# Where small corrections, operand splits and weight loads stand in the queues of a two-block transformer kernel

## The chip, the cores and the metric

The kernel runs as one program on one core of one Trainium2 chip. The metric is the device time in microseconds; several runs are summed up by their median. The core has a matrix engine (TensorE, PE in the profile; its weight loads are PEld), three engines for the rest (VectorE = DVE, ScalarE = ACT, GpSimd = POOL), and a queue engine (SyncE = SP) that here issues most transfers. Each engine runs its own queue in order.

## The reference, cut to what matters

One sequence of 1024 tokens, width 1024, float32, goes through two blocks. The first is a sliding-window attention layer and then a pooling layer; the second, which gets 16 meta tokens ahead of the sequence, has neighbourhood attention and a gated recurrence side by side, an output matrix `w_o`, and an MLP. Three places count here. The pooling layer:

```python
u, z = jnp.split(h @ w_in, [POOL_WIDTH], axis=-1)
p = multiscale_pool(u)
m = jnp.einsum('bsgc,gcd->bsgd', p, w_mix).reshape(B, S, POOL_WIDTH) * scale
return (m * jax.nn.silu(z)) @ w_out
```

`multiscale_pool` takes, in four groups of 256 channels, the mean over the last 2, 4, 8 or 16 tokens, and subtracts `u`. The first tokens have fewer than that behind them, so their sum is divided by their own count. After the layer come the residual sum, the norm that ends the first block, and the norm that begins the second. In the second block:

```python
y_hg = hgrn2_branch(q_hg, z_f, z_b, i_hg, g_hg, lb_all[:, l], hg_norm[l]) @ w_hg_out[l]
mix = jax.nn.sigmoid(gate_na) * y_na + jax.nn.sigmoid(gate_hg) * y_hg
h = h + mix @ w_o[l]
m = rms_norm(h, norm_mlp[l])
```

## The kernel before

**Products.** A float32 product is made of three products of rounded parts: each operand is split into hi (a cast, mostly on ScalarE) and lo (the operand less hi, on DVE or GpSimd). `split_evac` (L117 to 119) is one such pair for a 128x1024 piece; `split_w` (L79, L80) and `split_group` (L275, L276) split weights, with lo on GpSimd. A large matrix product is made as a Strassen-like scheme of 2x2 blocks, seven block products instead of eight; its sums of blocks (S1 to S4 of the left operand, differences of the weights) are made on DVE, and results are collected by copies and adds out of PSUM banks. A bank must be copied or added away before PE's later products can take it.

**Pooling projection** (`project_pairs`, with class `Pooled`, L866 on). Eight pairs of 128-column blocks, even pairs for `u` and odd ones for `z` of the same group. In a pair, PE makes six products of twelve 128x512 matmuls, by the blocks A11, A12, S2, S1, S3, S4 and A22 of the activations: the first bank is copied to SBUF by ScalarE (`copy`, L900), the next is added to it by DVE (`add`, through `vec`, L226), and so on; after the adds of odd pairs ScalarE applies Silu (L910). The pooling itself is done between these in small steps, a list `todo` from which `copy`, `add`, `opened` and `last` take the next: doubled sums over tokens (`doubled`, L226), then `less_u` (the mean less `u`, with a correction of the first 16 tokens: two DVE instructions of 128x16, `first` and its subtraction), then `cut` (the pooled half is split, hi on ScalarE at L118, lo on DVE at L119). `mix` multiplies a group's two pooled halves by `w_mix` and by Silu(z), stores the blocks (`d_mA...`) for the next product, and makes S1 to S4 of them; S3 is written over the block m[0,0], of which a store has been issued.

**Pooled output projection.** `times` makes 48 matmuls of one block product; the order is A11, A12, S2, S1, S4, S3, A22. `add_p` adds a finished bank to the residual rows `X` (DVE) and, where the rows are done, takes squares on ScalarE and multiplies by the gain. `second_norms` turns sums of squares into scales by Newton steps on small tiles (L124 to 132), `Rows.scale` scales rows alternately on DVE (L308) and ScalarE, and `turn_half` transposes scaled rows on PE (L282). The first four rows are done after the S4 product, so their scaling and transposes overlap with the S3 and A22 products. Ahead of that, the code splits the operands of the S3 product (`o7`) and of the last one (`o4` is A22, `t4` are its weights), normalises the meta tokens, and, between the transposes, splits gate weights (`wg`).

**The w_o stage** has the same plan. `mixed(e, hf)` loads two columns of w_hg, multiplies, and blends with the gates; the loop over e = 0, 2, 4, 6 makes the second half of them and the S1 and S3 blocks, and `load_w11` issues the first w_o weights in it. Then come the seven products; `add_x` (L1750 on) adds to `X`, whose halves the profile calls Xa and Xb.

**Order.** A list scheduler orders each engine's instructions when the program is built. `tc.issue_after(ins)` puts the instructions of its block that run on the engine of `ins` behind `ins` in that engine's queue; it does not change instructions on other engines.

Of the kernel before, what the change touches and what calls it, by code (L numbers as in the profile page):

```python
# [19 lines left out]
P = 128  # L20
# [10 lines left out]
def fused_kernel(tc, a, out, stop=None, dbg=None):  # L31
# [797 lines left out]
    with ExitStack() as ph:  # L829
# [34 lines left out]
        class Pooled:  # L864
# [33 lines left out]
            def copy(self, p, key, ps):  # L898
                c_ = ea[:, p - 2, :] if p in EARLY and key == "11" else self.dst(p, key)
                nc.scalar.copy(out=c_, in_=ps)  # L900
# [6 lines left out]
            def add(self, p, key, c_, ps):  # L907
                added[:] = [vec(c_, c_, ps, ALU.add)]
                if p % 2 and (p, key) != (3, "11"):
                    nc.scalar.activation(out=c_, in_=c_, func=AF.Silu)  # L910
# [3 lines left out]
            def last(self, p, ps):  # L914
# [5 lines left out]
                else:  # L920
                    nc.scalar.copy(out=c_, in_=ps)
                if p in EARLY:
# [9 lines left out]
            def pooled(self, g, j):  # L932
# [10 lines left out]
                def less_u():  # L943
                    pr, c_ = u[:, 16:], cur[-1]
                    first = small.tile([P, 16], F32, name="first", bufs=2)
                    vec(first, c_[:, 16:32], cnt[:, g, :], ALU.mult)
                    vec(pr[:, :16], first, u[:, 16:32], ALU.subtract)
# [3 lines left out]
                def cut():  # L951
                    self.pp[q][j] = s_tile(F32R)[:, :T], u_tile(F32R)[:, :T]
                    split_evac(*self.pp[q][j], u[:, 16:])
# [6 lines left out]
        def mix(g, q):  # L960
# [18 lines left out]
            for n, c_, x_, y_, op in (("S3", m[0, 0], m[0, 1], m[0, 0], ALU.subtract),  # L979
                                      ("S2", s2, m[1, 1], m[0, 0], ALU.add), ("S1", s1, m[0, 1], m[1, 1], ALU.add),  # L980
# [128 lines left out]
        with tc.issue_after(added[0].ins):  # L1109
            o7 = split_a("xl1", in_two(ring["S3"]))  # L1110
            o4 = split_a("xh1", in_two(ring["A22"]))
            mj = ea[:, 1:, :].rearrange("p a b -> p (a b)")
# [4 lines left out]
        ops = o7, split_b(w12)  # L1117
        t4 = list(zip(*[in_two(mp.tile([P, 4, 512], F32R, name=n, bufs=b)) for n, b in (("ub", 3), ("w22", 1))]))
        with tc.issue_after(made[0].ins):
            for i in range(2):  # L1120
                split_evac(*t4[i], w21[i])
        add_p(C, 0, 1, True)
        scaled = second_norms(0, 4)
        wg = []

        for n, ks in enumerate(((), (), (), (0, 1, 2), (3, 4), (5, 6), (7,), ())):
# [10 lines left out]
            if n in (1, 4):  # L1137
                wg.append(w_cols(w2, 4096 + len(wg) * P))
# [592 lines left out]
    with ExitStack() as ph:  # L1731
# [18 lines left out]
        def add_x(banks, h, ch, first=True, done=False, rows=range(4)):  # L1750

            for i in rows:
                t = 4 * h + i
                dst = X.at(t, ch)
                if first:
                    nc.vector.scalar_tensor_tensor(out=dst, in0=dst, scalar=rfin[:, t:t + 1], in1=banks[i], op0=ALU.mult,  # L1756
                                                   op1=ALU.add)
                else:
                    nc.vector.tensor_tensor(out=dst, in0=dst, in1=banks[i], op=ALU.add)
# [19 lines left out]
        for e in range(0, KT, 2):  # L1779
            if e == 6:  # L1780
                w11 = load_w11(wv)
            mixed(e, 1)
# [6 lines left out]
            if e == 4:  # L1789
                load_d(w21, wv, 1, 0)  # L1790
# [11 lines left out]
        o4 = split_a("xh1", in_two(a22))  # L1802
# [285 lines left out]
```

## Time and profile before

| | us |
|---|---|
| runs, median of 3 | 2376.18 (2375.15 to 2378.74) |
| profiled execution, whole time | 2372.9 |
| its span | 2371.1 |
| PE busy | 2277.2 |
| DVE busy | 1516.8 |
| ACT busy | 1021.4 |
| POOL busy | 776.1 |

The span is the time from the first to the last instruction in the profiled execution; the 1.8 us around it belong to the whole time. Busy is work of the engine itself, so a queue that stands still shows only as what is left. Starts below count from the span's begin. A row of the timeline has the start, the duration, the engine, the line of the kernel, the operation, out <- in, shapes and types, and in square brackets the time that the engine stood idle before it and what ended that. The pooling projection lies at about 505 to 660 us, the pooled output projection at 660 to 760, the w_o stage at 1600 to 1740.

### The profile page before, as it was taken

The numbers are of one execution on the slowest core, as the hardware profiler recorded it, in microseconds if no ns is written. First come the engines' busy times: TensorE is split into PE (matmuls) and PEld (weight loads), VectorE is DVE, ScalarE is ACT, GpSimd is POOL, SyncE is SP. The second block draws the span as 40 slices with busy tenths as digits, with TensorE's granted clock in tenths as the row PEclk, the third lists the DMA queues.
The fourth block names the chain that finished last, engine by engine and source line by source line (L and its number), as shares of the span: only waits on it lengthen the run. The fifth ranks groups of instructions, "written<-read, shape, count | busy, mean of one in ns | idle before, by whom it ended". The sixth has DMA issues, their size and how long they took to land. (4 is left out here: it accounts for less than half of the span.)

```text
span 2371.1 us, 32238 instructions
## 1 busy us (share of the span) xinstructions
PE 2277.2 (96%) x11910; PEld 1894.1 (80%) x11910; DVE 1516.8 (64%) x2740; ACT 1021.4 (43%) x1921; POOL 776.1 (33%) x519
## 2 busy tenths in 40 slices
PE   7999999988998999999999999999999999999997
PEld 6877777867776888888988888887778888878886
DVE  5566676798688355554166656668885444686775
ACT  5344452543355354544232322422475555533334
POOL 2112123343522254332222112114314444454455
PEclk9999999999999999999999999999999999999999
DMA  5111103423371222211111111358136444754231
GB/s 161 36 28 36 28 28 107 142 76 120 100 251 72 85 59 54 61 51 59 45 45 50 49 59 39 121 186 306 63 129 200 151 147 170 274 209 172 104 125 71
DMA packets 248941, 253.09 MB, mean 107 GB/s; under 512 B 61064, under 2 KB 183006, under 8 KB 244944
## 3 DMA queue, kind: packets, MB, share of 16 engines
q1 hardware_dynamic: 239968, 233.38, 30.2%
q10 hardware_dynamic: 8224, 16.00, 1.8%
q0 software_dynamic: 592, 1.65, 0.3%
q8 instruction: 94, 1.54, 0.3%
q14 instruction: 63, 0.52, 0.1%
HBM read 181.26 MB, written 69.46 MB: 106 GB/s over the span
## 5 line engine op out<-in xcount | busy, mean ns | idle before, releaser
L108 PE MATMUL mm<-xh,whi 128*128 128x512 f32 (+2 forms) x1616 | 622.0, 385 | 19.9 <-DVE z L226 6.2
L110 PE MATMUL mm<-xl,whi 128*128 128x512 f32 (+2 forms) x1616 | 615.2, 381 | 0.0
L111 PE MATMUL mm<-xh,wlo 128*128 128x512 f32 (+2 forms) x1616 | 612.8, 379 | 2.0 <-POOL wlo L80 2.0
L80 POOL TENSOR_TENSOR wlo<-wraw,whi 128x1024 fp32r<-128x1024 f32 (+1 forms) x99 | 234.6, 2373 | 751.9 <-ACT whi L79 644.5
L108 PEld LDWEIGHTS mm<-xh,whi 128*128 128x128 f32 x1616 | 305.7, 189 | 78.8 <-DVE z L226 7.0
L111 PEld LDWEIGHTS mm<-xh,wlo 128*128 128x128 f32 x1616 | 305.6, 189 | 60.7 <-POOL wlo L80 3.0
L110 PEld LDWEIGHTS mm<-xl,whi 128*128 128x128 f32 x1616 | 306.0, 189 | 50.8
L111 PE MATMUL mm<-whi,xl 128*128 128x512 f32 (+1 forms) x752 | 271.2, 361 | 0.0
L79 ACT CAST whi<-wraw 128x1024 fp32r<-128x1024 f32 (+1 forms) x99 | 101.1, 1022 | 265.4 <-PE mm L110 145.5
L110 PE MATMUL mm<-wlo,xh 128*128 128x512 f32 (+1 forms) x560 | 196.9, 352 | 2.7 <-POOL wlo L80 1.4
L108 PE MATMUL mm<-whi,xh 128*128 128x512 f32 (+1 forms) x560 | 196.6, 352 | 2.5 <-DVE x L527 1.0
L110 PE MATMUL mm<-wlo,xl 128*128 128x512 f32 x416 | 162.5, 391 | 7.3 <-POOL wlo L119 4.3
L108 PE MATMUL mm<-whi,xl 128*128 128x512 f32 x416 | 162.8, 391 | 6.0 <-DVE Xb L1756 2.4
L276 POOL TENSOR_TENSOR wlo<-raw,whi 128x1024 fp32r<-128x1024 f32 (+1 forms) x59 | 123.9, 2101 | 124.8 <-ACT whi L275 124.8
L111 PEld LDWEIGHTS mm<-whi,xl 128*128 128x128 f32 x752 | 141.8, 189 | 21.6
L110 PEld LDWEIGHTS mm<-wlo,xh 128*128 128x128 f32 x560 | 105.7, 189 | 17.8 <-POOL wlo L80 2.0
L108 PEld LDWEIGHTS mm<-whi,xh 128*128 128x128 f32 x560 | 105.8, 189 | 17.1 <-DVE x L527 1.4
L276 POOL TENSOR_TENSOR wlo<-wraw,whi 128x1024 fp32r<-128x1024 f32 (+1 forms) x28 | 69.0, 2466 | 135.0 <-ACT whi L275 96.6
L119 POOL TENSOR_TENSOR wlo<-wraw,whi 128x1024 fp32r<-128x1024 f32 x28 | 73.7, 2635 | 108.0 <-ACT whi L118 107.9
L108 PEld LDWEIGHTS mm<-whi,xl 128*128 128x128 f32 x416 | 78.1, 188 | 25.2 <-ACT whi L118 4.2
L110 PEld LDWEIGHTS mm<-wlo,xl 128*128 128x128 f32 x416 | 78.1, 188 | 25.1 <-POOL wlo L119 5.5
L2010 DVE TENSOR_TENSOR X<-X,mm 128x512 f32<-128x512 f32 x112 | 73.1, 681 | 38.2 <-PE mm L111 38.2
(436 smaller groups left out, 4581.7 us busy)
## 6 DMA issues: line engine op xcount, KB each, us to landing
wraw<-in_w_in_dram SPq DMA_DIRECT2D x48, 512.0 KB, 3.6
d_S<-st SPq DMA_DIRECT2D x64, 256.0 KB, 4.7
raw<-in_w_up_dram SPq DMA_DIRECT2D x30, 512.0 KB, 5.1
d_A<-st ACTq DMA_DIRECT2D x48, 256.0 KB, 2.0
fa<-d_S SPq DMA_DIRECT2D x10, 1024.0 KB, 4.7
fa<-d_A SPq DMA_DIRECT2D x9, 1024.0 KB, 4.8
wraw<-in_attn_w_in_dram SPq DMA_DIRECT2D x32, 256.0 KB, 3.0
xh<-in_w_down_dram SPq DMA_DIRECT2D x16, 512.0 KB, 5.4
```

The source lines that it names most:

```text
L79: nc.scalar.copy(out=hv[:, i:i + n], in_=view[:, i:i + n])
L80: nc.gpsimd.tensor_tensor(out=lv[:, i:i + n], in0=view[:, i:i + n], in1=f(hv[:, i:i + n]), op=ALU.subtract)
L108: nc.tensor.matmul(ps, lhsT=lh[0], rhs=rh[0], start=first and i == 0, stop=False, skip_group_check=chain)
L110: nc.tensor.matmul(ps, lhsT=lh[0], rhs=rh[1], start=False, stop=False, skip_group_check=chain)
L111: nc.tensor.matmul(ps, lhsT=lh[1], rhs=rh[0], start=False, stop=last and i == n - 1, skip_group_check=chain)
L119: return (lo_eng or nc.vector).tensor_tensor(out=lo, in0=src, in1=f(hi), op=ALU.subtract)
L276: nc.gpsimd.tensor_tensor(out=lv, in0=view, in1=f(hv), op=ALU.subtract)
L2010: added[:] = [nc.vector.tensor_tensor(out=dst, in0=dst, in1=banks[t], op=ALU.add)]
```

## The change

It touches three stages and no arithmetic.

*Pooling projection.* The two 128x16 corrections of `less_u` run on GpSimd instead of DVE (8 halves, so 16 instructions). `cut`'s ScalarE cast is queued behind the latest bank copy. S3 goes to a tile of its own. The Silu of pair 1's first block moves from the add to the pair's end.

*Pooled output projection.* The splits of the last product (`o4`, `t4`) move from ahead of the first rows' sums to behind them; the meta tokens' norm and the gate weights' splits are queued behind the scaling.

*w_o stage.* `mixed(6, 1)`, with its load, comes before `load_w11`; the splits `o4` and `t4` move behind the first rows' sums, and the DVE part of S3's operand split (`o7`) behind the adds of the product before.

```diff
             def copy(self, p, key, ps):
-                nc.scalar.copy(out=c_, in_=ps)
+                self.copied = nc.scalar.copy(out=c_, in_=ps).ins
...
-                if p % 2 and (p, key) != (3, "11"):
+                if p % 2 and (p, key) not in ((1, "11"), (3, "11")):
                     nc.scalar.activation(out=c_, in_=c_, func=AF.Silu)
...
+                if p == 1:
+                    c_ = self.dst(p, "11")
+                    nc.scalar.activation(out=c_, in_=c_, func=AF.Silu)
...
-                    vec(first, c_[:, 16:32], cnt[:, g, :], ALU.mult)
-                    vec(pr[:, :16], first, u[:, 16:32], ALU.subtract)
+                    nc.gpsimd.tensor_tensor(out=first, in0=c_[:, 16:32], in1=cnt[:, g, :], op=ALU.mult)
+                    nc.gpsimd.tensor_tensor(out=pr[:, :16], in0=first, in1=u[:, 16:32], op=ALU.subtract)
...
-                    split_evac(*self.pp[q][j], u[:, 16:])
+                    with tc.issue_after(self.copied):
+                        split_evac(*self.pp[q][j], u[:, 16:])
...
-            for n, c_, x_, y_, op in (("S3", m[0, 0], m[0, 1], m[0, 0], ALU.subtract),
+            s3 = s_tile()[:, :512]
+            for n, c_, x_, y_, op in (("S3", s3, m[0, 1], m[0, 0], ALU.subtract), ("S2", s2, m[1, 1], s3, ALU.add),
...
             o7 = split_a("xl1", in_two(ring["S3"]))
+        ops = o7, split_b(w12)
+        add_p(C, 0, 1, True)
+        with tc.issue_after(added[0].ins):
             o4 = split_a("xh1", in_two(ring["A22"]))
+            t4 = list(zip(*[in_two(mp.tile([P, 4, 512], F32R, name=n, bufs=b)) for n, b in (("ub", 3), ("w22", 1))]))
+            for i in range(2):
+                split_evac(*t4[i], w21[i])
+        scaled = second_norms(0, 4)
+        with tc.issue_after(scaled[1]):
             mj = ea[:, 1:, :].rearrange("p a b -> p (a b)")
...
-        ops = o7, split_b(w12)
-        t4 = list(zip(*[in_two(mp.tile([P, 4, 512], F32R, name=n, bufs=b)) for n, b in (("ub", 3), ("w22", 1))]))
-        with tc.issue_after(made[0].ins):
-            for i in range(2):
-                split_evac(*t4[i], w21[i])
-        add_p(C, 0, 1, True)
-        scaled = second_norms(0, 4)
...
-                wg.append(w_cols(w2, 4096 + len(wg) * P))
+                with tc.issue_after(scaled[0]):
+                    wg.append(w_cols(w2, 4096 + len(wg) * P))
...
         for e in range(0, KT, 2):
+            mixed(e, 1)
             if e == 6:
                 w11 = load_w11(wv)
-            mixed(e, 1)
...
-            if e == 4:
-                load_d(w21, wv, 1, 0)
+        load_d(w21, wv, 1, 0)
...
-        o4 = split_a("xh1", in_two(a22))
...
-        ops = split_a("xl1", in_two(a11)), split_b(w12)
-
-        t4 = list(zip(*[in_two(mp.tile([P, 4, 512], F32R, name=n)) for n in ("a22", "w22")]))
-        for i in range(2):
-            split_evac(*t4[i], w21[i])
+        with tc.issue_after(added[0].ins):
+            o7 = split_a("xl1", in_two(a11))
+        ops = o7, split_b(w12)
         wu0 = load_w(cols(w_up, 0))
         add_x(C, 0, 1, False, True)
+
+        with tc.issue_after(added[0].ins):
+            o4 = split_a("xh1", in_two(a22))
+            t4 = list(zip(*[in_two(mp.tile([P, 4, 512], F32R, name=n)) for n in ("a22", "w22")]))
+            for i in range(2):
+                split_evac(*t4[i], w21[i])
         scaled = X.norms(0, 4)
```

A scheduler sets the order on each engine, so the change shows best in what it makes of it. First ScalarE in the pooling projection, from the last copy of pair 6 on into pair 7 (`u` and `z` are the pairs' results, `sum` takes the hi part of a pooled half, `raw` and `wraw` are weights). Before:

```order
L921 COPY u<-mm 128x512
L900 COPY z<-mm 128x512
L118 CAST sum<-u 128x1024
L275 CAST whi<-raw 128x512
L910 ACTIVATE z<-z 128x512
L118 CAST sum<-u 128x1024
L900 COPY z<-mm 128x512
L79 CAST whi<-wraw 128x512
L900 COPY z<-mm 128x512
L910 ACTIVATE z<-z 128x512 x2
```

After:

```order
L921 COPY u<-mm 128x512
L900 COPY z<-mm 128x512
L275 CAST whi<-raw 128x512
L910 ACTIVATE z<-z 128x512
L900 COPY z<-mm 128x512
L79 CAST whi<-wraw 128x512
L900 COPY z<-mm 128x512
L118 CAST sum<-u 128x1024 x2
L910 ACTIVATE z<-z 128x512 x2
```

Both casts of the pooled halves now stand behind pair 7's three bank copies, where one stood behind the first copy and one directly ahead of the second.

Next DVE in the pooled output projection, after the adds into the last bank group that come ahead of the S3 operand's split (`xl1`; `xh1` is A22's operand, `w22` its weights, `mm` a bank, `sum` the gain; hx1, r1 and w1 are the meta tokens' norm). Before:

```order
L119 TENSOR_TENSOR xl1_6789<-ub_6590,xl1_6789 128x1024 x2
L119 TENSOR_TENSOR xh1_6794<-ub_6381,xh1_6794 128x1024 x2
L141 TENSOR_SCALAR hx1_6801<-ss_6799 16x1
L119 TENSOR_TENSOR w22_6822<-w21_6330,ub_6821 128x1024
L124 TENSOR_SCALAR r1_6802<-hx1_6801 16x1
L119 TENSOR_TENSOR w22_6822<-w21_6330,ub_6821 128x1024
L128 SCALAR_TENSOR_TENSOR w1_6803<-r1_6802,hx1_6801 16x1
L226 TENSOR_TENSOR raw_6369<-raw_6369,mm_6672 128x512
L132 SCALAR_TENSOR_TENSOR r1_6802<-w1_6803,r1_6802 16x1
L226 TENSOR_TENSOR raw_6370<-raw_6370,mm_6673 128x512
```

After:

```order
L119 TENSOR_TENSOR xl1_6793<-ub_6594,xl1_6793 128x1024 x2
L226 TENSOR_TENSOR raw_6372<-raw_6372,mm_6676 128x512
L226 TENSOR_TENSOR raw_6372<-raw_6372,sum_6438 128x512
L226 TENSOR_TENSOR raw_6373<-raw_6373,mm_6677 128x512
L226 TENSOR_TENSOR raw_6373<-raw_6373,sum_6438 128x512
L226 TENSOR_TENSOR raw_6374<-raw_6374,mm_6678 128x512
L226 TENSOR_TENSOR raw_6374<-raw_6374,sum_6438 128x512
L226 TENSOR_TENSOR raw_6375<-raw_6375,mm_6679 128x512
L119 TENSOR_TENSOR xh1_6826<-ub_6384,xh1_6826 128x1024
L226 TENSOR_TENSOR raw_6375<-raw_6375,sum_6438 128x512
L119 TENSOR_TENSOR xh1_6826<-ub_6384,xh1_6826 128x1024
L119 TENSOR_TENSOR w22_6832<-w21_6333,ub_6831 128x1024 x2
```

The four rows' sums stand directly behind the S3 operand's split; the last product's splits have gone behind them, and the token norm out of this place.

Last SyncE in the w_o stage, at the loads of the last w_hg columns and the first w_o weights (`st` holds gates and branch outputs). Before:

```order
L60 DMA wraw<-in_w_hg_out_dram 128x4x128 x2
L1743 DMA st<-d_gate 128x512
L1744 DMA st<-d_y 128x512
L232 DMA wraw<-in_w_o_dram 128x2x512 x2
L1743 DMA st<-d_gate 128x512
L60 DMA wraw<-in_w_hg_out_dram 128x4x128
L1744 DMA st<-d_y 128x512
L60 DMA wraw<-in_w_hg_out_dram 128x4x128
```

After:

```order
L60 DMA wraw<-in_w_hg_out_dram 128x4x128 x2
L1750 DMA st<-d_gate 128x512
L1751 DMA st<-d_y 128x512
L60 DMA wraw<-in_w_hg_out_dram 128x4x128 x2
L232 DMA wraw<-in_w_o_dram 128x2x512
L1750 DMA st<-d_gate 128x512
L232 DMA wraw<-in_w_o_dram 128x2x512
L1751 DMA st<-d_y 128x512
```

The last two w_hg loads now come ahead of the two w_o loads, and the second of these one transfer later.

More of the change, by code (lines that the diff above doesn't have):

```diff
@@ L978, in mix @@
             s2, s1 = [ring[n][:, 3, :] for n in ("S2", "S1")] if q == 3 else (s_tile()[:, :512], m[0, 1])
-            for n, c_, x_, y_, op in (("S3", m[0, 0], m[0, 1], m[0, 0], ALU.subtract),
-                                      ("S2", s2, m[1, 1], m[0, 0], ALU.add), ("S1", s1, m[0, 1], m[1, 1], ALU.add),
+            s3 = s_tile()[:, :512]
+            for n, c_, x_, y_, op in (("S3", s3, m[0, 1], m[0, 0], ALU.subtract), ("S2", s2, m[1, 1], s3, ALU.add),
+                                      ("S1", s1, m[0, 1], m[1, 1], ALU.add),
                                       ("S4", m[1, 0], m[1, 0], s2, ALU.subtract)):
@@ L1755, in add_x @@
                 if first:
-                    nc.vector.scalar_tensor_tensor(out=dst, in0=dst, scalar=rfin[:, t:t + 1], in1=banks[i], op0=ALU.mult,
-                                                   op1=ALU.add)
+                    added[:] = [nc.vector.scalar_tensor_tensor(out=dst, in0=dst, scalar=rfin[:, t:t + 1], in1=banks[i],
+                                                               op0=ALU.mult, op1=ALU.add)]
                 else:
-                    nc.vector.tensor_tensor(out=dst, in0=dst, in1=banks[i], op=ALU.add)
+                    added[:] = [nc.vector.tensor_tensor(out=dst, in0=dst, in1=banks[i], op=ALU.add)]
                 if done:
```

## The prediction

> **What bounds the kernel now.** I read the page's engine table first, then TensorE's waits over the whole span, then the clock by stretches, and last the timelines of the waits in the three stages that the change touches. The engine table of the page gives busy time and share:
>
> ```profile
> span 2371.1 us, 32238 instructions
> PE 2277.2 (96%) x11910; PEld 1894.1 (80%) x11910; DVE 1516.8 (64%) x2740; ACT 1021.4 (43%) x1921; POOL 776.1 (33%) x519
> ```
>
> TensorE (PE) works 96% of the time, and its work stays the same here. So the change can only gain PE's idle time, and matmuls at a lowered clock. The PE waits give: who waits, for whom, total us, how often, the longest.
>
> ```profile
> PE mm L108 <- DVE z L226: 7.1, 3, 3.9
> PE mm L108 <- ACT z L900: 6.9, 2, 3.9
> PE mm L282 <- DVE raw L308: 5.5, 1, 5.5
> PE mm L108 <- DVE u L226: 3.4, 2, 1.7
> PE mm L110 <- DVE wlo L119: 3.3, 3, 1.8
> PE mm L108 <- DVE Xb L1756: 2.4, 2, 1.7
> PE mm L108 <- ACT whi L79: 2.3, 1, 2.3
> PE mm L111 <- POOL wlo L80: 2.0, 2, 1.7
> ```
>
> These rows hold 32.9 us. The z and u rows are the pooling projection, where a product waits until a bank of the one before is copied or added away; raw is the pooled output projection, whose transposes wait for normed rows; wlo on DVE, Xb, whi and wlo on POOL are mostly the w_o stage. A long wait costs more than itself, which the windows show (stretch, length, busy us and count of PE, weight load, DVE, ACT, POOL, then granted clock, DMA share, GB/s):
>
> ```profile
> 525.00:535.00 10.00, 7.05 (x24) 5.68 (x25) 9.93 (x13) 5.42 (x7) 4.08 (x3) 0.83 0.00 1
> 600.00:610.00 10.00, 8.68 (x38) 7.24 (x39) 5.31 (x8) 5.37 (x8) 3.86 (x3) 1.00 0.36 101
> 653.00:660.00 7.00, 5.12 (x16) 4.10 (x17) 1.98 (x4) 2.54 (x4) 1.88 (x2) 0.76 0.56 173
> 745.00:757.00 12.00, 7.38 (x34) 6.51 (x35) 10.65 (x21) 6.68 (x13) 2.29 (x1) 0.72 0.18 54
> 1634.00:1645.00 11.00, 7.95 (x27) 6.13 (x28) 8.59 (x9) 3.46 (x4) 6.95 (x4) 0.84 0.68 242
> ```
>
> After an idle of 3.9 us (first and third row) the clock is 0.83 over 10 us and 0.76 over 7: 10 x 0.17 or 7 x 0.24, 1.7 us of work lost each time. The 3.0 us idle of the second row left it at 1.00. The last row holds two shorter waits (2.3 and 1.7) close together and loses 11 x 0.16 = 1.8.
>
> **Pooling projection: three edits.** Their rows, DVE and ScalarE (ACT) and GpSimd (POOL) by start, duration, operation, and the wait ahead of it:
>
> ```profile
> 519.85 3.31 POOL L276 TENSOR_TENSOR wlo<-wraw,whi 128x1024 fp32r<-128x1024 f32 x1 [3.54 <-ACT whi L275]
> 520.83 2.37 DVE L226 TENSOR_TENSOR first<-sum,cnt 128x16 f32<-128x16 f32 x1
> 545.02 2.45 DVE L226 TENSOR_TENSOR z<-z 128x512 f32<-128x512 f32 x1 [2.00 <-DMA d_mA<-z]
> 566.87 0.50 PE L108 MATMUL mm<-xh,whi 128*128 128x512 f32 x1 [2.27 <-DVE z L226]
> 576.90 0.50 PE L110 MATMUL mm<-u,whi 128*128 128x512 f32 x1 [0.83 <-DVE u L119]
> 584.78 1.67 DVE L226 TENSOR_TENSOR z<-z 128x512 f32<-128x512 f32 x1 [2.85 <-DMA d_mA<-z]
> 599.74 1.04 ACT L118 CAST sum<-u 128x1024 fp32r<-128x1024 f32 x1 [5.45 <-DVE u L226]
> 600.69 0.58 ACT L900 COPY z<-mm 128x512 f32<-128x512 f32 x1
> 653.30 1.04 ACT L118 CAST sum<-u 128x1024 fp32r<-128x1024 f32 x1 [0.70 <-DVE u L226]
> 654.25 0.58 ACT L900 COPY z<-mm 128x512 f32<-128x512 f32 x1
> L838 POOL TENSOR_SCALAR cnt<-cnt 128x16 f32<-128x16 f32 x4 | 1.0, 252 | 0.2
> ```
>
> *Casts behind copies.* At 599.74 ScalarE had waited 5.45 us in its queue for a pooled half, and the bank copy of pair 5 stood behind it, with PE's next product. Tied behind the copy, the cast no longer blocks it: the wait of 3.0 in the 600 to 610 window goes, +3.0. Pair 7 has the same pattern at 653.30: without that cast the copy can run at about 652, once the Silu ahead of it, which waits for DVE's sum of the other bank, is done. Of its 3.9 I take 2.5 and leave 1.4; a wait of 1.4 should not pull the clock down where 3.0 did not, so of the 1.7 lost I take +1.6 besides. What waits instead is the cast, with the ScalarE work queued behind it (for pair 7 the two Silus and the casts of the next stage's operands); the mix that reads it has the rest of its pair's products in front of it.
>
> *S3 into a tile of its own.* The subtraction at 545.02 overwrote a block whose store was still under way (2.00 of waiting, then 2.45 running), and DVE's queue behind it holds the sum that frees pair 2's bank; at 584.78 it is 2.85, for pair 4. The u row's two waits (3.4 in sum) follow. With a free tile the subtraction starts when its inputs are there, at least 2.0 sooner, and the sum is then bounded by its own matmuls. I take +1.3 of each 1.7, +2.6, and nothing for pair 6, where the u row has no third wait. Bounds are 0 (the new tile waits for a slot instead) and 3.4. The Silu of pair 1 that moves to the pair's end costs nothing: ScalarE is busy 5.42 of the 10 us there.
>
> *Corrections on GpSimd.* Sixteen DVE instructions go, sixteen come to GpSimd. On DVE one of 128x16 could take 2.37, as at 520.83, because a GpSimd weight subtraction was running (519.85, 3.31 long). On GpSimd the nearest row is 0.25 (L838, the same size); the far bound is a weight subtraction's 3.31. I take 0.25. In pair 3 the corrections then stand ahead of the next weight subtraction, and the sum that ends the 2.27 at 566.87 comes about 1.9 sooner: +1.9. The mix waits 0.83 and a little before it; with the halves ready earlier, +1.1. In pair 1 (the 3.9) GpSimd and DVE alternate on their corrections and sums and nothing is saved: its wait and its clock stay, −0.5. Behind the corrections on GpSimd's queue stand weight subtractions, which PE needs only in the next pair.
>
> [...]
>
> Sum here: 3.0 + 2.5 + 1.6 + 2.6 + 1.9 + 1.1 − 0.5 = **12.2**; bounds from 5 (casts alone) to 15.
>
> **Pooled output projection.** DVE rows around the last two products:
>
> ```profile
> 724.82 2.34 DVE L119 TENSOR_TENSOR xh<-ub,xh 128x1024 fp32r<-128x1024 f32 x2
> 729.62 0.67 DVE L226 TENSOR_TENSOR raw<-raw,mm 128x512 f32<-128x512 f32 x1
> 742.48 0.69 DVE L226 TENSOR_TENSOR raw<-raw,sum 128x512 f32<-128x512 f32 x1 [1.54 <-ACT ea L1045]
> 744.97 2.33 DVE L131 TENSOR_TENSOR w<-w,hx 128x8 f32<-128x8 f32 x1
> 748.82 1.41 DVE L308 TENSOR_SCALAR raw<-raw,r 128x1024 f32<-128x1024 f32 x2
> ```
>
> The first rows' sums (729.62) stand behind two splits for the last product (724.82, 1.17 each) and, with the token norm, two more among them. And a 128x8 step of the Newton iteration took 2.33 at 744.97, where a whole 128x512 sum takes 0.69 (742.48): GpSimd was subtracting the gate weights that the change ties behind the scaling. With four splits (4 x 1.17 = 4.7) behind the sums and at least 1.6 (2.33 − 0.69) off the iteration, 6.3 in all, the scaling at 748.82 can start 5 sooner, at about 743.8, with 1.3 left for the sums' own wait on PE. The wait of 5.5 ends, +5.5. Of the 3.4 us of clock in the 745 to 757 window (12 x 0.28) I credit half a drop, +0.9, since PE goes on in short pieces there. The splits serve the last product, which starts one product of 48 matmuls later (8.68 / 38 = 0.23 each, 11 us): 4.7 fit. The gate weights, now behind the scaling, are used only after that last product, another 11 us: nothing. Sum **6.4**, bounds 2 (the squares on ScalarE, 1.54 of waiting at 742.48, still end last) to 9.
>
> **The w_o stage.** SyncE's issues, then the work:
>
> ```profile
> 1618.73 2.02 SPq L232 DMA_DIRECT2D wraw<-in_w_o_dram  x2
> 1627.73 0.37 SPq L60 DMA_DIRECT2D wraw<-in_w_hg_out_dram  x1
> 1634.24 1.05 ACT L79 CAST whi<-wraw 128x1024 fp32r<-128x1024 f32 x1 [9.85 <-DMA wraw<-in_w_hg_out_dram]
> 1650.59 4.54 DVE L119 TENSOR_TENSOR xh<-a,xh 128x1024 fp32r<-128x1024 f32 x2
> 1685.43 6.59 DVE L119 TENSOR_TENSOR xl<-fa,xl 128x1024 fp32r<-128x1024 f32 x3
> 1691.94 0.73 DVE L1756 SCALAR_TENSOR_TENSOR Xb<-Xb,rfin,mm 128x512 f32<-128x512 f32 x1
> 1696.34 1.21 DVE L119 TENSOR_TENSOR w<-st,a 128x1024 fp32r<-128x1024 f32 x1
> 1704.96 0.69 DVE L1759 TENSOR_TENSOR Xa<-Xa,mm 128x512 f32<-128x512 f32 x1 [2.03 <-PE mm L111]
> 1709.41 1.41 DVE L308 TENSOR_SCALAR Xa<-Xa,r 128x1024 f32<-128x1024 f32 x2
> ```
>
> *Loads.* The last w_hg weights were issued at 1627.73, behind the w_o load of 1618.73, and cast at 1634.24 after 9.85 of waiting. In w_o's place they leave 9 us sooner, and the waits of 2.3 (whi) and 1.7 (wlo) go: +4.0, and the clock of the last window, +1.6. Late next: the first w_o weights, two transfers that now leave one tile later, with a whole half product ahead of their use. [...]
>
> *Splits.* Xb's sums (1691.94) waited behind three splits of 6.59; two of these now follow: the 2.4 of the Xb row go. The xh1 splits leave the queue at 1650.59 (4.54), behind which DVE's weight splits come; of the 3.3 that PE waits for those, I take 1.2, a little over a third. The next product's operand, split later, may cost 0.3. [...] Sum 4.0 + 1.6 + 2.4 + 1.2 − 0.3 − 1.5 = **7.4**, bounds 3 to 10.
>
> Total 12.2 + 6.4 + 7.4 = **26.0**. The profiled execution took 2372.9, so 2346.9; it lies 3.3 below the median of the runs, 2376.2, and from that the forecast is **2350**.
>
> **The rivals.**
> 1. *The waits are passed on.* A freed sum only meets the next queue: pair 7's Silu, GpSimd's subtractions. For it: DVE is at 9.93 of 10 in the first window. Against: 5.31 and 1.98 in the two windows of the casts. Half of the pooling gain and 2 elsewhere go: 26 − 8 = 18, **2358**. Chance 0.20.
> 2. [...] Chance 0.12.
> 3. [...] Chance 0.05.
> 4. *It doesn't do what it says*: the scheduler and the queues hide it, e.g. SyncE issues the w_hg load no sooner since its tile is not free, and the remaining waits close up: **2376**. Against: two casts and a load plainly stand behind others now. Chance 0.04.
>
> **How the numbers follow.** Forecast 0.59, with its own bounds of 5 + 2 + 3 = 10 to 15 + 9 + 10 = 34 if all fell together; they won't, so 26 ± 9. About 0.2% (4.75 us) is what a measurement of this kernel can tell from no change. Range: from 26 + 8 (2342) to rival 1 with its own error of 8 (2366). Faster 0.59 + 0.20 + 0.12 = 0.91; same 0.04; slower 0.05.
>
> **What would show it.** In the profile after: no PE wait on z's copy (L900) near 600, one of 1.4 near 652, the clock there at 1.00; raw L308 gone from the list of waits; whi L79 and Xb gone in w_o, a new one on Xa's transposes of 1 to 2.5; no DMA wait ahead of S3; POOL corrections of about 0.25. Wrong if corrections take over 1.6, if DVE's sums still come where they came, or if PE's busy time rises.

## The result

The changed kernel took 2355.7 us (median of 4 runs, 2354.5 to 2357.1), the kernel before 2375.7 (4 runs, 2374.2 to 2378.7). The ratio is 0.9915, with a 95% interval of 0.9897 to 0.9932: 20 us faster. The forecast was 2350, so 26 us were forecast and 20 came. Its signs and most of its mechanisms held; several sizes did not.

The page of the changed kernel, against the two rows that the prediction begins with:

```profile
span 2354.9 us, 32237 instructions
PE 2281.8 (97%) x11910; PEld 1900.3 (81%) x11910; DVE 1504.1 (64%) x2724; ACT 1020.2 (43%) x1921; POOL 785.5 (33%) x535
```

The span lost 16.2 us in this pair of profiled runs, which lie 2.8 below and 1.0 above the medians of their kernels. PE's busy time rose by 4.6, at the same number of matmuls. The prediction had called such a rise a sign of being wrong, but it is no more work: the matmuls in the stretches at half clock kept PE busy for nearly twice as long (in this profile, 128x512 matmuls 0.43 us from start to start between 481 and 485, 0.23 between 471 and 475), and it met more of them. The granted clock was at half for 48.6 us against 42.5, and PE was busy in 35.5 of these against 27.4; half of that difference is 4.0 of the 4.6. PE's waits now (who waits, for whom, total us, how often, the longest):

```profile
PE mm L108 <- DVE z L226: 5.2, 3, 3.7
PE mm L110 <- DVE wlo L119: 3.3, 3, 1.8
PE mm L108 <- ACT whi L118: 3.2, 3, 1.7
PE mm L111 <- POOL u L881: 2.5, 1, 2.5
PE mm L282 <- DVE u L308: 1.9, 1, 1.9
...
PE mm L108 <- ACT z L900: 1.0, 1, 1.0
PE mm L108 <- DVE u L226: 1.0, 2, 0.8
...
PE mm L282 <- DVE Xa L308: 0.6, 1, 0.6
```

Gone are the 5.5 for raw, 5.9 of the 6.9 for z's copies, 2.4 of the 3.4 for u, and the rows of Xb, whi (L79) and, all but 0.2, wlo (L80). New are a wait of 1.9 for the last rows' scaling (u L308), one of 0.6 for Xa, 0.8 more for whi (L118), and 2.5 for "u L881", which has to do with chance and not with the change, as will be seen.

To see where the time came from, the span is cut at events that every trace has. The stretches are the pooling projection with the end of the stage ahead of it (first row), the last three products of the pooled output projection up to the gates' first results (second), and the w_o stage (third). Before, then after (stretch, length, busy of PE, weight load, DVE, ACT, POOL, the granted clock, DMA):

```profile
477.90:671.70 193.80, 172.78 (x729) 137.64 (x729) 150.17 (x166) 75.79 (x109) 75.05 (x42) 0.98 0.38 118
717.00:795.00 78.00, 66.14 (x312) 53.66 (x312) 58.12 (x113) 41.20 (x83) 17.96 (x8) 0.96 0.26 92
1594.00:1747.70 153.70, 142.06 (x636) 114.99 (x636) 123.87 (x160) 67.37 (x102) 50.22 (x21) 0.99 0.49 171
```

```profile
478.90:664.20 185.30, 174.43 (x728) 139.99 (x728) 146.64 (x150) 75.70 (x109) 89.19 (x56) 0.96 0.36 112
707.60:782.20 74.60, 67.32 (x313) 54.95 (x313) 56.88 (x113) 41.21 (x84) 18.08 (x8) 0.95 0.27 96
1583.40:1731.50 148.10, 139.98 (x637) 113.89 (x637) 118.74 (x160) 66.79 (x103) 45.46 (x21) 1.00 0.51 178
```

8.5, 3.4 and 5.6 us came from these three, and 1.9 from the 45 us between the first and the second (671.7 to 717.0 before is 45.3 long, 664.2 to 707.6 after 43.4): 19.4. The rest of the span, which the change does not touch, took 3.2 back in this profile. The measured 20 agrees with the sum of the stages; that this pair of profiles shows 16.2 is luck.

Part of that luck can be read in the clock. Ahead of 478 the two programs run the same code and both then have an idle of 2.3 us; before (first fence) the clock stayed at 1.00, after (second) it fell to 0.76 over 14 us:

```profile
476.00:490.00 14.00, 11.36 (x50) 9.09 (x51) 14.00 (x23) 9.39 (x16) 4.02 (x2) 1.00 0.84 225
```

```profile
477.00:491.00 14.00, 11.78 (x39) 9.22 (x40) 12.43 (x21) 8.17 (x14) 4.03 (x2) 0.76 0.87 225
...
528.00:538.00 10.00, 7.23 (x19) 5.73 (x20) 9.93 (x10) 4.37 (x6) 4.18 (x6) 0.66 0.00 0
...
1729.00:1749.00 20.00, 16.68 (x62) 12.74 (x61) 18.13 (x30) 14.32 (x24) 4.77 (x2) 0.83 0.45 136
```

14 x 0.24 = 3.4, 10 x 0.34 = 3.4, 20 x 0.17 = 3.4. The rows of before that the prediction quotes give 1.7 (525), 1.7 (653), 3.4 (745) and 1.8 (1634). The loss came in portions of 1.7 us, one or two at a time, and the wait of 2.3 at 478 cost none of them before and two after. In the table below the clock's share of a stretch is added up from short windows in the same way.

### The profile page after: what moved, and what is told of

It reads as the page before. It is cut to its first block, busy times and chain, and to the rows that moved or that the text cites. A ratio compares the mean times of both kernels' runs of the same rounds, so it can differ in the third digit from the quotient of the medians.

```text
span 2354.9 us, 32237 instructions
## 1 busy us (share of the span) xinstructions
PE 2281.8 (97%) x11910; PEld 1900.3 (81%) x11910; DVE 1504.1 (64%) x2724; ACT 1020.2 (43%) x1921; POOL 785.5 (33%) x535
## 4 chain that ended last, share of the span: by engine, by line
PE 60%; DVE 11%; issue 3%; DMA 2%; ACT 2%; POOL 1%; SPq 0%; DVEq 0%; ACTq 0%; POOLq 0%
PE mm L110 18%; PE mm L108 18%; PE mm L111 18%; PE A L1550 2%; PE PT L1314 1%; DVE xl L119 1%; PE S L1291 1%; DVE sum L226 1%; PE tp L1570 1%; DVE raw L226 1%; DVE s L1303 1%; DVE xh L119 0%; DMA st<-d_y 0%; ACT ea L1050 0%; PE mm L282 0%
## 5 line engine op out<-in xcount | busy, mean ns | idle before, releaser
L80 POOL TENSOR_TENSOR wlo<-wraw,whi 128x1024 fp32r<-128x1024 f32 (+1 forms) x99 | 233.7, 2364 | 738.1 <-ACT whi L79 673.7
L79 ACT CAST whi<-wraw 128x1024 fp32r<-128x1024 f32 (+1 forms) x99 | 101.1, 1022 | 258.1 <-PE mm L110 146.0
L119 POOL TENSOR_TENSOR wlo<-wraw,whi 128x1024 fp32r<-128x1024 f32 x28 | 73.7, 2636 | 108.9 <-ACT whi L118 86.9
```

Source lines behind the costliest of these rows:

```text
L79: nc.scalar.copy(out=hv[:, i:i + n], in_=view[:, i:i + n])
L80: nc.gpsimd.tensor_tensor(out=lv[:, i:i + n], in0=view[:, i:i + n], in1=f(hv[:, i:i + n]), op=ALU.subtract)
L119: return (lo_eng or nc.vector).tensor_tensor(out=lo, in0=src, in1=f(hi), op=ALU.subtract)
```

## The experiments

Each of the first eight puts one part of the change back or repeats the change; the last four alter it. They ran on three chips in groups of four; the kernel before took 2375.8, 2374.3 and 2372.2 us there (9 to 11 runs each), so "gain" is against the kernel before on the same chip. The intervals of the ratios are about ±0.13%, or 3 us, wide, so that two gains can differ by some 4 us by chance; the lengths of the stages tell finer. "Pooling", "output" and "w_o" are the three stretches of above, in us, and behind each in brackets what the lowered clock took of it.

| kernel | time | gain | ratio, 95% interval | pooling | output | w_o |
|---|---|---|---|---|---|---|
| before (first profile) | 2375.7 | | | 193.8 (3.4) | 78.0 (3.4) | 153.7 (1.7) |
| changed (first profile) | 2355.7 | 19.9 | 0.9915, 0.9897 to 0.9932 | 185.3 (6.8) | 74.6 (3.4) | 148.1 (0) |
| changed_again | 2354.2 | 20.1 | 0.9913, 0.9901 to 0.9926 | 184.1 (5.1) | 74.6 (3.4) | 149.0 (1.7) |
| casts_untied | 2363.5 | 12.3 | 0.9952, 0.9939 to 0.9964 | 193.2 (10.2) | 74.3 (1.7) | 148.9 (1.7) |
| corr_on_dve | 2359.2 | 16.7 | 0.9937, 0.9922 to 0.9952 | 189.5 (6.8) | 74.2 (1.7) | 150.1 (3.4) |
| s3_in_place | 2358.2 | 17.6 | 0.9927, 0.9915 to 0.9939 | 187.4 (6.8) | 74.2 (1.7) | 149.0 (1.7) |
| pool_out_before | 2358.7 | 17.1 | 0.9931, 0.9918 to 0.9945 | 182.2 (1.7) | 77.9 (3.4) | 149.6 (1.7) |
| wo_before | 2357.8 | 16.5 | 0.9924, 0.9912 to 0.9937 | 185.5 (5.1) | 74.2 (1.7) | 153.7 (1.7) |
| wo_load_before | 2356.6 | 17.7 | 0.9926, 0.9914 to 0.9938 | 182.6 (3.4) | 74.6 (1.7) | 152.4 (3.4) |
| gates_untied | 2355.9 | 18.4 | 0.9919, 0.9908 to 0.9931 | 185.2 (6.8) | 74.5 (1.7) | 150.9 (3.4) |
| norm_later | 2351.3 | 20.9 | 0.9911, 0.9897 to 0.9926 | 182.7 (3.4) | 70.7 (0) | 151.0 (3.4) |
| wo_splits_later | 2353.8 | 18.3 | 0.9923, 0.9911 to 0.9936 | 184.4 (5.1) | 74.6 (1.7) | 150.0 (3.4) |
| pair1_add_first | 2353.5 | 18.6 | 0.9924, 0.9911 to 0.9937 | 181.3 (1.7) | 74.6 (3.4) | 149.0 (1.7) |
| all_three | 2348.7 | 23.5 | 0.9901, 0.9888 to 0.9915 | 185.4 (6.8) | 70.7 (1.7) | 149.8 (3.4) |

Eight profiles share the changed kernel's pooling code: 182.2 to 185.5, 184.0 in the mean. Without the clock's share they lie between 178.3 and 180.5. So this stage is known to about 1 us once the clock is taken off, and to 2 with it. The output stretch behaves otherwise. Nine profiles have its changed code (all but before, pool_out_before, gates_untied, norm_later and all_three), and it is 74.2 to 74.6 long in each of them: three lost two portions there, and the six that lost only one have a wait of 1.0 to 1.1 more. There a portion that is not lost is not time gained.

### The change once more: changed_again

> The changed kernel itself once more, on the same chip as the next three, as their reference. Its first profile had granted clocks of 0.5 to 0.6 for some 7 us behind a 2.3 us idle at 478, where the kernel before had 1.00 behind the same idle. If that drop is chance (the code up to there is the same), some of this kernel's runs are about 3 us faster, near 2353, and the median lies between 2353 and 2357. If it belongs to the change, the same drop stands in this profile too.

2354.2 (2352.6 to 2354.7). The lowered clock behind 478 stood in this profile again, but with one portion instead of two (1.7). Of the other kernels eight, among them norm_later (1.7) and gates_untied (3.4), had one or two there; pool_out_before, with the same code up to there, had none, like the kernel before. So it is chance, though none is the rarer case; the last section shows where the wait fell in the profiles before and after.

### The casts: casts_untied

```diff
-                    with tc.issue_after(self.copied):
-                        split_evac(*self.pp[q][j], u[:, 16:])
+                    split_evac(*self.pp[q][j], u[:, 16:])
```

> The changed kernel without the tie of the pooled halves' ScalarE casts behind the bank copy, everything else kept. Forecast's theory: the tie bought 3.0 at pair 5, 2.5 at pair 7 and 1.6 of clock behind pair 7, so 7.1 us slower than the changed kernel (about 2363), with PE waits of about 3 at pair 5's S2 and 3.5 to 3.9 at pair 7's S3 product, both for the z copy of L900, and a granted clock below 0.9 after the second. Rival (the waits are passed on by DVE's queue, and the tie alone does little): under 3.5 us slower, with the two waits under 2 each.

7.7 less gain than the changed kernel; the forecast had 7.1. Both waits come back, for the copy of z:

```profile
599.61 0.51 PE L108 MATMUL mm<-s2h,whi 128*128 128x512 f32 x1 [2.09 <-ACT z L900]
...
654.47 0.50 PE L108 MATMUL mm<-s3h,whi 128*128 128x512 f32 x1 [3.56 <-ACT z L900]
```

Without the lowered clock the stage is 183.0, 4.2 longer than the changed kernel's mean of the two profiles (178.8); the rest of its 193.2 is clock, 10.2 against 5.1 and 6.8, with a portion behind each of the two waits, the one of 2.1 too. So the waits were worth 4.2, where 5.5 was forecast, and the clock 3.4, where 1.6 was. The mechanism is shown; that the sum is met so closely is partly luck.

### The corrections: corr_on_dve

```diff
-                    nc.gpsimd.tensor_tensor(out=first, in0=c_[:, 16:32], in1=cnt[:, g, :], op=ALU.mult)
-                    nc.gpsimd.tensor_tensor(out=pr[:, :16], in0=first, in1=u[:, 16:32], op=ALU.subtract)
+                    vec(first, c_[:, 16:32], cnt[:, g, :], ALU.mult)
+                    vec(pr[:, :16], first, u[:, 16:32], ALU.subtract)
```

> The changed kernel with the sixteen corrections of less_u back on DVE, everything else kept. Forecast's theory: they bought 1.9 at pair 3's A22 product and 1.1 at the mix and cost 0.5 at pair 1, so this kernel should be 2.5 us slower than the changed one (about 2358), with the wait before pair 3's A22 product back at 2 to 2.3 us from 1.0. [...] A trace of the changed kernel adds a doubt about pair 1: there a GpSimd weight subtraction started behind the corrections and held up a DVE weight sum for 2.85 us; with the corrections on DVE that sum should take 0.7 again.

3.4 less gain; the stage is 4 to 5 longer (189.5), 3.9 without the clock. The wait ahead of pair 3's A22 product is back, and larger than before the change:

```profile
568.25 0.53 PE L108 MATMUL mm<-xh,whi 128*128 128x512 f32 x1 [3.39 <-DVE z L226]
...
605.01 0.50 PE L108 MATMUL mm<-s3h,whi 128*128 128x512 f32 x1 [1.46 <-ACT z L900]
...
651.60 0.50 PE L108 MATMUL mm<-s3h,whi 128*128 128x512 f32 x1 [2.34 <-ACT z L900]
```

So the move bought time, though some of the corrections are long on GpSimd too. How they fare there in the changed kernel:

```profile
522.82 1.15 POOL L949 TENSOR_TENSOR first<-sum,cnt 128x16 f32<-128x16 f32 x1 [3.53 <-DVE sum L226]
...
564.20 3.43 POOL L949 TENSOR_TENSOR first<-sum,cnt 128x16 f32<-128x16 f32 x1 [5.26 <-DVE sum L226]
567.71 0.22 POOL L950 TENSOR_TENSOR u<-first,u 128x16 f32<-128x16 f32 x1
```

Of the sixteen, eight took 0.21 or 0.22, seven 1.06 to 1.24, one 3.43: mean 0.83. Beside the one of 3.43, which ends at 567.6, DVE ran a row of 128x1008 to 128x1039 sums from 564.05 on, and its next instruction, an add that reads a bank, started at 567.5. Nor have they become much shorter: before the change the sixteen took 0.16 to 2.37 on DVE, 0.90 in the mean. But what stands behind them on GpSimd is a weight split, and PE waits for none of these between 500 and 660, whereas on DVE they stood in front of the sums that free PE's banks.

### S3: s3_in_place

```diff
-            s3 = s_tile()[:, :512]
+            s3 = m[0, 0]
```

> The changed kernel with S3 written over its block again, everything else kept. Forecast's theory: the free tile bought 1.3 at each of two A22 products (pairs 2 and 4), so 2.6 us slower than the changed kernel, with DVE waiting 2 to 3 us for a store ahead of S3 and PE waits of about 1.5 at both products. Rival (the sum waits for its own matmuls or for DVE anyway): no difference over 1 us, and the two waits at 0.2 and 0.8 as in the changed kernel.

2.4 less gain. The waits ahead of the A22 products of pairs 2 and 4 are 1.7 and 2.8, against 0.2 and 0.7 to 0.8 in the two profiles of the changed kernel (the second is 0.7 to 1.5 in the others with its pooling code):

```profile
552.50 0.50 PE L108 MATMUL mm<-xh,whi 128*128 128x512 f32 x1 [1.69 <-DVE u L226]
...
589.54 0.79 PE L108 MATMUL mm<-xh,whi 128*128 128x512 f32 x1 [2.80 <-DVE u L226]
```

Not all of it stays: pair 3's wait of 1.0 is not there, the mix waits 0.6 for 1.1, and without the clock the stage is 180.6, 1.8 longer than the changed kernel's 178.8. And the stretch from this stage to the output's last products is 44.8 here, 43.4 in the changed kernel, with waits of 0.7 and 0.9 that the changed kernel has not or at 0.5. The free tile saved 1.4 there too, which no step had forecast.

### The output projection put back: pool_out_before

This puts the operand splits, the token norm and the gate weights of the pooled output projection where they were.

> The changed kernel with the whole pooled output projection as before, everything else kept. Forecast's theory: 6.4 us slower (about 2362), with the 5.5 us wait of the transposes for the scaled rows back. The trace of the changed kernel shows a new wait of 1.9 us for the last row's scaling behind the gate products; if that is the change's own cost (token norm and gate weights now lie among the last adds), it is gone here, and the net is 5.9 minus nothing. Rival (the transposes' wait is only moved on to the last rows): under 3 us slower.

```profile
703.20:781.10 77.90, 65.95 (x313) 53.59 (x313) 58.05 (x113) 41.16 (x84) 17.97 (x8) 0.96 0.26 92
```

77.9 against 74.6: 3.3, not 6.4, and 2.9 by time. The 5.5 us wait is back (735.85, raw L308), with two portions of lowered clock; the wait of 1.9 at the last rows is not there. That the change brings a wait of its own here was right. What makes it is asked by the next two.

### Who makes the new wait: gates_untied and norm_later

```diff
-                with tc.issue_after(scaled[0]):
-                    wg.append(w_cols(w2, 4096 + len(wg) * P))
+                wg.append(w_cols(w2, 4096 + len(wg) * P))
```

> The changed kernel with the gate weights' splits no longer queued behind the scaling, the token norm still behind it. The forecast priced the tie at nothing. From the changed kernel's trace: GpSimd's two weight subtractions (2.4 each) there hold up a 16x1 step (2.15) and the 16x1024 scaling (2.55) of the token norm on DVE, and the last row's scaling comes 1.9 late. If the tie makes that wait, it is gone here, and a Newton step of the first rows takes 2.3 again, with the first transposes later by about 1: 0 to 2 us faster. If the token norm makes it, the wait of 1.9 stays, and this kernel is the same or 1 to 2 slower.

In the changed kernel the tie looks guilty: a small step of the token norm and its scaling took 2.15 and 2.55 us on DVE, beside GpSimd's weight subtractions of 2.39 and 2.40, and the last row is scaled late.

```profile
735.67 2.39 POOL L80 TENSOR_TENSOR wlo<-wraw,whi 128x1024 fp32r<-128x1024 f32 x1 [10.89 <-ACT whi L79]
735.91 2.15 DVE L132 SCALAR_TENSOR_TENSOR r<-w,r 16x1 f32<-16x1 f32 x1
...
741.17 2.40 POOL L80 TENSOR_TENSOR wlo<-wraw,whi 128x1024 fp32r<-128x1024 f32 x1 [3.12 <-ACT whi L79]
...
741.57 2.55 DVE L1129 TENSOR_SCALAR sum<-sum,r 16x1024 f32<-16x1024 f32 x1
```

Untying them brought the wait down from 1.9 to 0.3, but others of 0.4 and 1.0 came in its place, and the stretch is as long (74.5). One step of the token norm still takes 2.2 there (at 737.05), beside a weight subtraction that runs from 736.80 on. Moving the norm instead, behind the stage's last add and after its loop:

```diff
-        with tc.issue_after(scaled[1]):
-            mj = ea[:, 1:, :].rearrange("p a b -> p (a b)")
...
+        with tc.issue_after(added[0].ins):
+            mj = ea[:, 1:, :].rearrange("p a b -> p (a b)")
```

> The changed kernel with the meta tokens' norm moved from behind the first rows' scaling to behind the last add of the stage. Theory: the norm's small steps, each of which could wait for a GpSimd weight subtraction, delayed the last rows' adds, and with them the last scaling; without them the 1.9 us wait there goes, and now and then a lowered clock behind it: 2 to 3 us faster than the changed kernel. Rival (the gate weights' subtractions would hold up any DVE work there, or the norm's steps now delay the last Newton iteration): the wait stays over 1, same time within 1.

```profile
704.20:774.90 70.70, 64.48 (x312) 52.05 (x312) 55.42 (x113) 41.00 (x84) 18.06 (x8) 1.00 0.28 101
```

70.7: 3.9 shorter, in this stretch, than the changed kernel, and free of a lowered clock in this run. all_three has the same edit and again 70.7, with one portion of lowered clock. Against the changed kernel's two profiles, 1.0 of the 3.9 is idle time of PE in norm_later and the rest clock; in all_three 1.9 is idle time. The wait of 1.9 (last scaling) is gone, and one of 1.1 for a transposed half (xl L322), which five of these kernels show between the transposes (gates_untied among them), is 0.2. What the norm cost can be read on DVE. Its nine instructions there, eight small steps and the scaling, took 5.9 us in the changed kernel, 4.7 of them in the two rows shown above; these end at 738.06 and 744.12, the weight subtractions beside them at 738.06 and 743.57. In norm_later, where GpSimd does nothing beside them, the nine took 2.1, with the scaling at 0.74:

```profile
750.97 0.74 DVE L1148 TENSOR_SCALAR sum<-sum,r 16x1024 f32<-16x1024 f32 x1
```

So the cost was the norm's place beside the gate weights' splits, in a queue that the rows' adds share. Moving the norm away is enough; untying the splits is not. By time, norm_later gains 20.9 on its chip against 20.1 and 19.9: a difference that the times alone can't show.

### The w_o stage put back: wo_before and wo_load_before

wo_before has the whole stage as before; wo_load_before only this:

```diff
-            mixed(e, 1)
             if e == 6:
                 w11 = load_w11(wv)
+            mixed(e, 1)
```

> The changed kernel with the whole w_o stage as before. Forecast's theory: 7.4 us slower than the changed kernel. From the changed kernel's trace: waits of 2.3 and 1.7 at the last mixed products and 1.7 and 0.7 at Xb back, one of 1.1 and one of 1.2 ahead of two split weights gone, and the 0.6 at the transposes gone: 2.3 + 1.7 + 2.4 - 1.1 - 1.2 - 0.6 = 3.5, and 1.8 of clock: 5.3. Rival (the gains pass on to the next wait): under 3.

153.7 against 148.1 and 149.0, and 3.6 less gain than changed_again: 4.7 to 5.6, by the stretch, nearer the 5.3 read from the trace than the 7.4 of the forecast.

> The changed kernel with only the order of the w_hg and w_o loads as before. Forecast's theory: 4.0 of idle back and a lowered clock behind it, 5.6 us slower than the changed kernel, less what the earlier w_o loads save. If two idles of 2.3 and 1.7, neither of them long, don't lower the clock, 4.0. Rival: the w_o weights' own splits then come sooner and the 1.2 and 1.1 us waits of the changed kernel at 1645 and 1652 go, so only 4.0 + 1.7 - 2.3 = 3.4.

152.4, 3.4 more than changed_again, of which 1.7 is clock; 2.4 less gain. The waits of the load, in this kernel, and those that the changed kernel has instead:

```profile
1620.24 0.50 PE L108 MATMUL mm<-xh,whi 128*128 128x512 f32 x1 [1.67 <-ACT whi L79]
1622.69 0.79 PE L111 MATMUL mm<-xh,wlo 128*128 128x512 f32 x1 [1.71 <-POOL wlo L80]
...
1654.33 0.50 PE L110 MATMUL mm<-wlo,xl 128*128 128x512 f32 x1 [1.62 <-DVE wlo L119]
```

```profile
1645.39 0.50 PE L110 MATMUL mm<-wlo,xl 128*128 128x512 f32 x1 [1.24 <-DVE wlo L119]
...
1652.56 0.50 PE L108 MATMUL mm<-whi,xl 128*128 128x512 f32 x1 [1.66 <-ACT whi L118]
1654.83 0.49 PE L110 MATMUL mm<-wlo,xl 128*128 128x512 f32 x1 [1.77 <-DVE wlo L119]
```

The rival's mechanism was the right one: with the load in time PE comes earlier to the next products, whose weights are split at the pace they had. Of the 4.0 that the load cost before the change, 2.3 meet PE again in this profile: a wait of 1.2 that was not there, and 1.7 where it was 0.6. The second stands in every profile with this code, the first is anything up to 1.4 and in some under 0.3. That the rival's 3.4 was met to the tenth is luck, since 1.7 of it is clock, for which it had no term.

### Three edits on top of the change

wo_splits_later puts the split of the last product's weights out of the Newton iteration, behind the scaling:

```diff
             o4 = split_a("xh1", in_two(a22))
+        scaled = X.norms(0, 4)
+        with tc.issue_after(scaled[1]):
             t4 = list(zip(*[in_two(mp.tile([P, 4, 512], F32R, name=n)) for n in ("a22", "w22")]))
             for i in range(2):
                 split_evac(*t4[i], w21[i])
-        scaled = X.norms(0, 4)
```

> The changed kernel with the two splits of the last w_o product's weights behind the scaling of the first rows, out of the Newton iteration. Theory: the transposes' wait of 0.6 us goes, with up to 1 us of spread around it; the splits are ready before the last product: 0.5 to 1 faster, hard to tell by time, to be seen in the trace. Rival: the splits are late for the last product and PE waits 1 or more for them there.

The 0.6 us wait of the transposes is gone and no other has come; without the clock's share the stage is 146.6, against 147.3 to 148.1 in the changed kernel. But corr_on_dve, with the wait and the same w_o code as the changed kernel, has 146.7, so a gain is not shown, and the time, 18.3 of gain, shows none either.

pair1_add_first ties pair 1's pooling steps behind the sum that frees its bank:

```diff
+                if p == 1 and key == "22":
+                    with tc.issue_after(added[0].ins):
+                        self.steps()
-                if p % 2 and key != "11":
+                elif p % 2 and key != "11":
                     self.steps()
```

> The changed kernel with pair 1's later pooling steps queued behind the sum that frees the bank for its last product. Theory: the 3.7 us wait before that product comes from four DVE steps that stand ahead of the sum, one of them held up by a GpSimd weight subtraction (2.85); with the sum first the wait falls under 1, and no lowered clock (0.5 for some 4 us) follows: 2.8 + 1.7 to 3.4 = 4.5 to 6 us faster than the changed kernel. Rival (the steps are only moved and the mix of the first group waits for its halves, or pair 2's sums wait): under 2 faster, with waits of 2 to 3 between 550 and 580.

The 3.7 us wait is gone, and the clock stays up there. In its place the first group's mix waits:

```profile
535.21 0.74 PE L108 MATMUL mm<-sum,whi 128*128 128x512 f32 x2 [2.26 <-ACT sum L118]
536.95 0.50 PE L110 MATMUL mm<-u,whi 128*128 128x512 f32 x1 [1.00 <-DVE u L119]
```

3.3 of 3.7 are given back within 5 us: the rival's case. What it saves is the clock, when it saves it: 1.7 was lost in this stretch, but 6.8 in all_three, which has the same edit and two portions behind the new wait.

> The changed kernel with the three last edits together (token norm later, w_o weight splits later, pair 1's sum first). Theory: their sum, 7 to 10 us faster than the changed kernel, 2346 to 2349. Rival (each gain is taken back by the next wait): under 4.

2348.7 (2348.0 to 2349.7) is the fastest kernel measured, 23.5 below the kernel before on its chip. The interval of its ratio overlaps the changed kernel's, so that it beats the kernel before is shown, and that it beats the changed one is shown in the output stretch (70.7) and not by the time. The expected 7 to 10 did not come. By gain it is 3.5; the output stretch gives 3.9, and the other two stretches (185.4 and 149.8) are as long as in the changed kernel.

## Why the prediction was right, and where its sizes were off

- **What bounds the kernel.** Right: all that was gained is PE's idle time and clock, and every stage's gain is made up of its waits and its clock.
- **Casts behind copies.** Right: the 3.0 at pair 5 went, 3.9 at pair 7 fell to 1.0 (1.4 was left in the sum), and the clock stays at 1.00 behind it. casts_untied gives 7.7 back; 7.1 was forecast, with two errors that cancel: the waits were worth 4.2 for 5.5, the clock 3.4 for 1.6.
- **S3.** Right: 1.7 to 0.2 and 1.7 to 0.8, 2.4 in all (2.6), of which s3_in_place gives 1.8 back in this stage. It also gave 1.4 later, through no step of the prediction.
- **Corrections.** The sign was right, the terms were not. Pair 3 gained 1.3 (1.9 was forecast). "The mix waits 0.83 and a little before it; with the halves ready earlier, +1.1" failed: it still waits 1.07, for the same split (u L119). Yet put back on DVE they cost 3.4 by time, more than their 2.5: pairs 5 and 7 then wait 1.5 and 1.3 more as well, which the prediction had not in its sum. "On GpSimd the nearest row is 0.25" was low: 0.83 in the mean. The mark of 1.6 each, at which the sixteen would use up the forecast 26 (26 / 16), was not reached, and the 13 us that the sixteen do take on GpSimd (16 x 0.83) are not on PE's path: it waits for none of GpSimd's work between 500 and 660. In pair 1 nothing was lost, 3.7 of waiting for 3.9.
- **Pooled output projection.** "+5.5" was right, and the splits' cover held. The half drop of clock, "+0.9", did not come in the two profiles of the changed kernel (3.4 lost, as before). "The gate weights, now behind the scaling, are used only after that last product: nothing" looked for the weights' user and not for who shares their engine and queue; the token norm that moves with them had no price at all. Beside each other they brought a wait of 1.9. That is 6.4 forecast and 3.4 measured; norm_later shows that 7.3 was there.
- **w_o.** The wait of the loads went ("+4.0"), and Xb's 2.4. But the step "of the 3.3 that PE waits for those, I take 1.2" misread its row and had the wrong sign. Of the row's 3.3 only 1.8 (at 1669.26) lies in w_o; 1.2 and 0.3 lie in the pooled output projection, at 694.27 and 671.66. And w_o's share grew by one of 1.2, and the one for whi ahead of it by 1.1, since PE came earlier to weights that are split no earlier. And "+1.6" for the clock came in one of two profiles only, by luck: behind the waits at 1652 and 1654 the clock fell again in changed_again and in all nine other kernels that have them. No run shows the term "−1.5" for the transposes; the changed kernel's list of waits has 0.6 there, and more than that is not shown. Of 7.4, 4.7 to 5.6 came.
- **Sum.** 12.2 + 6.4 + 7.4 = 26 was forecast; the stretches give 9.8 (by the mean of 184.0) + 1.9, 3.4 and 4.7 to 5.6, 20 to 21; the 1.9, between two stages, is in no step of the prediction. Rival 1, with 18, came nearer to the 20 than the forecast with 26, and its mechanism, waits passed on to the next queue, is what w_o's loads and the further edit of pair 1 show. It is not what the change met in the pooling projection, where most of it had been placed. Not tried alone were the Silu that moves in pair 1, priced at nothing, and w_o's splits.

## What to carry to other kernels

Price a moved instruction by who stands behind it in its new queue, and by what the other engines run beside it there, as well as by who needs its result: the token norm was needed much later, its scaling took 2.55 us beside a weight subtraction and 0.74 without one, and it still cost up to 4 us. A wait taken away ahead of a stage that is itself just in time is worth what the next supplier has in hand (2.3 of w_o's 4.0 came back, 3.3 of pair 1's 3.7), so read the next two waits on the same chain before adding up the first. And where the clock's losses differ from run to run by several portions, compare stage by stage, with the clock's share and without it, before believing a few microseconds.

## What the runs showed of the hardware

The lost clock came in portions: over 14 profiles, in the three stages, the sum of length x (1 - granted clock) behind a wait was 0, 1.7 or 3.4 us, nothing between. The length of a wait alone doesn't settle whether one follows: waits of 2.1 (casts_untied at 599.6) and 1.9 (changed kernel at 724.8) were followed by a lowered clock, while 3.0 at 601.3 before the change was not, and the same 2.3 at 478 was followed by none (before and pool_out_before), one (norm_later, all_three and others) or two portions (changed kernel, gates_untied) in runs of the same code.

Where the wait falls does, nearly, in the profiles before and after. In both the clock is at half for 3.41 or 6.83 us (but for the last microseconds of the program), and in each these stretches start on one grid of 3.413 us, to within 0.01 us: before, the first and the last of them start 2344.96 us apart, 687 steps of that grid. Nine of the other profiles, in windows of 3 us, fit such a grid to 0.03 us. Cut along the grid of its own profile, the 3.0 us wait before the change falls into two windows (first two rows: PE busy 1.68 and 2.12 of 3.41), and the 2.1 us wait of casts_untied into one (last two rows: busy 1.32, then half clock):

```profile
596.62:600.03 3.41, 1.68 (x8) 1.03 (x6) 3.41 (x3) 0.29 (x1) 3.05 (x1) 1.00 0.00 0
600.03:603.44 3.41, 2.12 (x9) 1.80 (x10) 3.41 (x6) 1.26 (x3) 0.00 (x0) 1.00 0.52 154
...
597.32:600.73 3.41, 1.32 (x6) 0.94 (x6) 2.22 (x2) 1.53 (x2) 3.41 (x3) 1.00 0.00 0
600.73:604.14 3.41, 3.41 (x10) 2.64 (x9) 2.82 (x4) 1.49 (x3) 1.81 (x2) 0.50 0.53 154
```

In the profiles before and after, cut this way from end to end, 13 of these windows at full clock have PE idle for 1.9 us or more, and half clock followed every one; it followed 1 of the 8 with 1.6 to 1.8 idle, 2 of the 60 with 0.6 to 1.6, and none of the others. The grid lies differently in time from run to run, which is the chance at 478: before, the idle time there fell into two windows with 1.55 and 1.49, after, into one with 2.21.

The lowered clock behind 478 came with a longer wait behind it, too. In the changed kernel GpSimd's next weight split started 0.06 behind a DVE split (493.06, 493.00) instead of 0.23 ahead of it (490.44, 490.67 before) and took 4.0 instead of 2.4, and PE's wait for it was 2.5 instead of 1.7 (the row "u L881" in the list of waits). Seven more kernels have that wait of 2.5; in norm_later and wo_load_before, with a lowered clock there as well, PE waited 0.8.
